# A decoder block on one core: the MLP's down product by seven quarter-block products instead of eight

## The chip, the cores and the metric

The kernel runs on one core of one Trainium2 chip. The metric is the device time of one execution in microseconds (us), taken as a median over runs. TensorE multiplies into PSUM, VectorE and ScalarE do the elementwise work and can read PSUM, GpSimd does elementwise work on SBUF alone, and SyncE issues most of the loads.

## The reference

```python
def reference(x, ...):                       # x: 1 x 256 x 2048, float32
    h = rms_norm(x, g_mix); proj = h @ w_in  # q k v r lr cb cc cx ga gb
    ...                                      # gated linear attention, short convolution
    x = x + merged @ w_o
    h2 = rms_norm(x, g_ffn)
    hid = square(relu(h2 @ w_ffn_up))        # 256 x 8192
    x = x + hid @ w_ffn_down                 # 8192 x 2048
    return rms_norm(x, g_final)
```

Only the last three lines and the norm are touched by the change.

## The kernel before, in words

Every matrix product runs in split float32: an operand is cast to the matmul's own float format (`hi`), the rest is kept as `lo = x - hi`, and the product is the sum of hi·hi, hi·lo and lo·hi. So each weight tile is loaded by SyncE (1 MB), cast in two halves of 128x1024 by ScalarE (L52), and VectorE subtracts to get `lo` (L53); five `whi` and five `wlo` buffers let both run ahead of TensorE.

The MLP works in four quarters of 2048 hidden columns (L610). For each of 16 blocks of 128 hidden columns, `ws_product` (L57) multiplies one up weight tile with the 16 activation tiles `B`: 16 matmuls of 512 columns and 16 of 256. `total` (L75) then adds main part and correction: ScalarE copies the correction out of PSUM (L78), VectorE adds (L79), squares the positive part (L614), and the result is split again into the tile `A[i]` (L86, L87). After 16 blocks `xs_product` (L129) multiplies the quarter by the down weights: for each of four column groups of 512, 16 blocks x 2 token halves x 3 matmuls of 512 columns (L415 to L417), two PSUM banks at a time. `down_evac` (L586) adds a bank to the residual `xtok` with one VectorE instruction (L589). The last column group of the last quarter is done one token half at a time (L644), followed by the final norm and the store.

The order on each engine is made by a scheduler that reorders the instructions of the program by its own priorities; a pool with n buffers limits how far a producer runs ahead. GpSimd does nothing but set four constants.

Of the kernel before, what the change touches and what calls it, by code (L numbers as in the profile page):

```python
# [20 lines left out]
GATE_NORM = 16.0  # L21
LEVELS = (4, 8, 16, 32, 64)
NM = len(LEVELS) * 64 + 128 + 3 * 64
NQ = 4


@with_exitstack
def block_kernel(ctx, tc, xT, wq, wk, wlr, wv, wr, wcb, wcc, wcx, wga, wgb, wgu,
# [557 lines left out]
    def down_evac(ps, m, c0, w, k):  # L586

        xs = xtok[:, m, c0:c0 + w]
        nc.vector.scalar_tensor_tensor(out=xs, in0=ps, scalar=rs2[:, m:m + 1], in1=xs, op0=ALU.mult, op1=ALU.add)  # L589
        if k is not None:  # L590
            jk = mp.tile([P, 512], F32, tag="junk", name="jk")
            nc.scalar.activation(jk[:, :w], xs, AF.Square, accum_out=ssq[:, m, k:k + 1])
            if k < 3:
                nc.vector.tensor_mul(out=xs, in0=xs, in1=gf[:, c0:c0 + w])

    def final_norm(m):
        nc.vector.tensor_reduce(out=sqf[:, m:m + 1], in_=ssq[:, m, :4 + m], op=ALU.add, axis=mybir.AxisListType.X)
        nc.vector.tensor_scalar(out=msf[:, m:m + 1], in0=sqf[:, m:m + 1], scalar1=1.0 / D, scalar2=EPS,
                                op0=ALU.mult, op1=ALU.add)
        rf = rsqrt_mean(msf[:, m:m + 1], [P, 1], "rf", 2)  # L600
        for c in range(4):
            xs = xtok[:, m, c * 512:(c + 1) * 512]
            if c < 3:
# [4 lines left out]
            nc.sync.dma_start(out=out[m * P:(m + 1) * P, c * 512:(c + 1) * 512], in_=xs)

    for qd in range(NQ):  # L610
        for i in range(KT):
# [1 line left out]
            hid = tmp("t1")
            nc.vector.scalar_tensor_tensor(out=hid, in0=s, scalar=0.0, in1=s, op0=ALU.max, op1=ALU.mult)  # L614
            split_act(A[i], hid)
        final = qd == NQ - 1
        for c in range(4):
            if final and c == 3:
                break
# [7 lines left out]
    for kg in range(4):
        src = wdown[((NQ - 1) * 4 + 3) * 4 + kg]  # L630
        if kg < 2:
            st = wst.tile([P, 2048], F32, tag="wst", name="wst_t")
            nc.sync.dma_start(out=st, in_=src)
            for kk in range(4):
                hi, lo = B[(kg * 4 + kk) * 2], B[(kg * 4 + kk) * 2 + 1]
                ws = st[:, kk * 512:(kk + 1) * 512]
                nc.scalar.copy(out=hi, in_=ws)
                nc.vector.tensor_sub(out=lo, in0=ws, in1=hi.bitcast(F32))
                wres.append((hi, lo))
        else:  # L640
            for hi, lo in wsplit(src):
                for kk in range(2):
                    wres.append((hi[:, kk * 512:(kk + 1) * 512], lo[:, kk * 512:(kk + 1) * 512]))
    for m in range(2):  # L644
        for c0, cw_ in ((0, 512),) if m == 0 else ((0, 256), (256, 256)):
            ps = mmp.tile([P, cw_], F32, tag="mm", name="ps_xs")
            for kt in range(KT):
# [1 line left out]
                ah = A[kt][:, m * P:(m + 1) * P]
                al = A[kt][:, T + m * P:T + (m + 1) * P]  # L650
                nc.tensor.matmul(ps, lhsT=ah, rhs=hi[:, c0:c0 + cw_], start=(kt == 0), stop=False)  # L651
                nc.tensor.matmul(ps, lhsT=ah, rhs=lo[:, c0:c0 + cw_], start=False, stop=False)  # L652
                nc.tensor.matmul(ps, lhsT=al, rhs=hi[:, c0:c0 + cw_], start=False, stop=(kt == KT - 1))  # L653
# [77 lines left out]
```

## Time and profile before

| | us |
|---|---|
| median of 3 runs (1757.11 to 1757.98) | 1757.19 |
| the profiled execution | 1757.05 |
| its span, first to last instruction | 1755.1 |
| TensorE busy in it | 1739.9 |
| VectorE / ScalarE / GpSimd busy | 1117.4 / 834.5 / 0.2 |

A busy time is the sum of an engine's instruction durations; matmul ends are modelled and matmuls overlap, so the rate of TensorE is read from start to start or from the length of a stretch. The granted clock was 1.00 in the stretches shown below.

### The profile page before, as it was taken

The page shows a single profiled execution, that of the slowest core. Times are in us where ns is not written, and L with a number is a line of the kernel's source. Part 1 is how long each engine was busy: PE and PEld are TensorE (multiplying, and loading weights), DVE is VectorE, ACT ScalarE, POOL GpSimd, SP SyncE. Part 2 cuts the span into 40 slices and gives each one's busy share as a digit, 9 for nine tenths or more (in the row PEclk, how much of TensorE's full clock was granted, in tenths as well). Part 3 has the DMA queues.
Part 4 walks back from the last instruction along what each step waited for, and adds up shares of the span by engine and source line. Part 5 has one row for each costly group of instructions (what it writes and reads, how often), then busy time and mean ns, then how long its engine had stood idle before and what let it go on. Part 6 is the DMA issues. An engine that isn't in the chain of part 4 may idle for free.

```text
span 1755.1 us, 22568 instructions
## 1 busy us (share of the span) xinstructions
PE 1739.9 (99%) x8988; PEld 1479.5 (84%) x8988; DVE 1117.4 (64%) x1597; ACT 834.5 (48%) x1098; POOL 0.2 (0%) x4
## 2 busy tenths in 40 slices
PE   8999999999999999999999999999999999999998
PEld 6888888888888888888888888888888888888887
DVE  8978888665544448864556666555665566556664
ACT  7745454444344446654444555434443444335451
POOL 0000000000000000000000000000000000000000
PEclk9999999999999999999999999999999999999999
DMA  8454444455555554465555555555555555555552
GB/s 314 168 192 169 168 168 168 169 191 192 192 192 192 192 192 148 171 211 195 193 191 202 205 188 192 190 193 192 186 179 196 193 184 191 192 192 192 186 191 79
DMA packets 74726, 328.72 MB, mean 187 GB/s; under 512 B 5693, under 2 KB 7869, under 8 KB 44158
## 3 DMA queue, kind: packets, MB, share of 16 engines
q1 hardware_dynamic: 71952, 323.55, 52.1%
q10 hardware_dynamic: 2670, 3.74, 0.6%
q8 instruction: 70, 1.15, 0.3%
q14 instruction: 34, 0.28, 0.0%
HBM read 325.17 MB, written 2.10 MB: 186 GB/s over the span
## 4 chain that ended last, share of the span: by engine, by line
PE 99%; DMA 0%; DVE 0%; ACT 0%; SPq 0%; issue 0%; DVEq 0%; ACTq 0%
PE ps_mm L70 34%; PE ps_mm L72 16%; PE ps_xs L415 8%; PE ps_xs L416 8%; PE ps_xs L417 8%; PE ps_xb L417 7%; PE ps_xb L415 7%; PE ps_xb L416 7%; PE ps_mm L69 1%; PE sp L289 1%; PE ps_mm L177 1%; PE ps_xs L652 0%; PE ps_xs L651 0%; PE ps_xs L653 0%; PE po L471 0%; PE ps_mm L179 0%
## 5 line engine op out<-in xcount | busy, mean ns | idle before, releaser
L53 DVE TENSOR_TENSOR wlo<-wst_t,whi 128x1024 fp32r<-128x1024 f32 x470 | 575.1, 1224 | 309.5 <-ACT whi L52 304.2
L52 ACT CAST whi<-wst_t 128x1024 fp32r<-128x1024 f32 x470 | 493.8, 1052 | 429.4 <-PE ps_xs L417 230.0
L70 PE MATMUL ps_mm<-A,whi 128*128 128x512 f32 x1488 | 527.1, 399 | 0.0
L72 PE MATMUL ps_mm<-A,wlo 128*128 128x256 f32 x1395 | 392.6, 281 | 0.0
L70 PE MATMUL ps_mm<-B,whi 128*128 128x512 f32 x1024 | 357.5, 399 | 0.0
L70 PEld LDWEIGHTS ps_mm<-A,whi 128*128 128x128 f32 x1488 | 275.8, 188 | 58.5
L72 PE MATMUL ps_mm<-B,wlo 128*128 128x256 f32 x960 | 269.7, 281 | 0.0
L72 PEld LDWEIGHTS ps_mm<-A,wlo 128*128 128x128 f32 x1395 | 263.3, 189 | 2.7
L442 DVE TENSOR_TENSOR wlo<-wst_t,whi 128x1024 fp32r<-128x1024 f32 x128 | 156.8, 1225 | 170.7 <-ACT whi L441 170.5
L415 PE MATMUL ps_xs<-whi,A 128*128 128x512 f32 x608 | 236.5, 389 | 0.0
L416 PE MATMUL ps_xs<-wlo,A 128*128 128x512 f32 x608 | 236.5, 389 | 0.0
L417 PE MATMUL ps_xs<-whi,A 128*128 128x512 f32 x608 | 236.5, 389 | 0.0
L70 PEld LDWEIGHTS ps_mm<-B,whi 128*128 128x128 f32 x1024 | 188.4, 188 | 41.7
L441 ACT CAST whi<-wst_t 128x1024 fp32r<-128x1024 f32 x128 | 134.8, 1053 | 184.6 <-PE ps_xb L417 174.6
L72 PEld LDWEIGHTS ps_mm<-B,wlo 128*128 128x128 f32 x960 | 181.3, 189 | 3.1
L78 ACT COPY corr<-ps_mm 128x256 f32<-128x256 f32 x144 | 53.6, 372 | 221.8 <-PE ps_mm L70 220.9
L417 PEld LDWEIGHTS ps_xs<-whi,A 128*128 128x128 f32 x608 | 114.2, 188 | 23.8
L415 PEld LDWEIGHTS ps_xs<-whi,A 128*128 128x128 f32 x608 | 114.2, 188 | 23.6
L416 PEld LDWEIGHTS ps_xs<-wlo,A 128*128 128x128 f32 x608 | 114.2, 188 | 23.5
L79 DVE TENSOR_TENSOR t<-ps_mm,corr 128x256 f32<-128x256 f32 x144 | 60.9, 423 | 108.2 <-ACT corr L78 107.6
L415 PE MATMUL ps_xb<-whi,A 128*128 128x512 f32 x256 | 99.9, 390 | 0.0
L415 PE MATMUL ps_xb<-whi,B 128*128 128x512 f32 x256 | 99.8, 390 | 0.0
(188 smaller groups left out, 1564.4 us busy)
## 6 DMA issues: line engine op xcount, KB each, us to landing
wst_t<-in_wup SPq DMA_DIRECT2D x64, 1024.0 KB, 4.8
wst_t<-in_wdown SPq DMA_DIRECT2D x64, 1024.0 KB, 4.8
wst_t<-in_wcc SPq DMA_DIRECT2D x16, 1024.0 KB, 4.8
wst_t<-in_wcx SPq DMA_DIRECT2D x16, 1024.0 KB, 4.8
wst_t<-in_wcb SPq DMA_DIRECT2D x16, 1024.0 KB, 4.8
wst_t<-in_wv SPq DMA_DIRECT2D x16, 1024.0 KB, 4.7
wst_t<-in_wgb SPq DMA_DIRECT2D x16, 1024.0 KB, 5.0
wst_t<-in_wconv SPq DMA_DIRECT2D x16, 1024.0 KB, 5.0
```

The lines of the kernel that those rows point to most:

```text
L52: nc.scalar.copy(out=hi, in_=s)
L53: nc.vector.tensor_sub(out=lo, in0=s, in1=hi.bitcast(F32))
L69: nc.tensor.matmul(ps[:, T:], lhsT=lo[:, sl], rhs=act[kt][:, :T], start=False, stop=False)
L70: nc.tensor.matmul(ps, lhsT=hi[:, sl], rhs=act[kt], start=(kt == 0), stop=last)
L72: nc.tensor.matmul(ps[:, T:], lhsT=lo[:, sl], rhs=act[kt][:, :T], start=False, stop=False)
L78: nc.scalar.copy(out=c, in_=corr)
L79: nc.vector.tensor_add(out=out_t, in0=main, in1=c)
L415: nc.tensor.matmul(pss[m], lhsT=ah, rhs=hi, start=(kt == 0), stop=False)
L416: nc.tensor.matmul(pss[m], lhsT=ah, rhs=lo, start=False, stop=False)
L417: nc.tensor.matmul(pss[m], lhsT=al, rhs=hi, start=False, stop=(kt == n - 1))
L441: nc.scalar.copy(out=hi, in_=sh)
L442: nc.vector.tensor_sub(out=lo, in0=sh, in1=hi.bitcast(F32))
```

## The change

The MLP now goes in eight pieces of 1024 hidden columns. For pieces 1 to 7 the down product is made of *units*: a unit is 512 hidden columns (`d`) by 1024 output columns (`g`), four units a piece. Left operand (256 tokens x 512), right operand (512 x 1024) and result are cut in 2x2 quarter blocks, and a unit is seven products of quarter blocks, 6 matmuls of 512 columns each, where eight would be needed otherwise. The seven need sums of quarter blocks. Of the right side (`s_tiles`) they are `x1`, `x2`, an in-place sum in the loaded tile, and `x4`, each 128x1024 and made by GpSimd. Of the left side (`combos`) they are four, each 128x256, by GpSimd. The seven results lie in seven PSUM banks, and after the two units of a `g` they are combined into `xtok` (`s_evac`): VectorE and ScalarE read the banks, GpSimd does five additions of 128x512.

Between the seven products of a unit stand two up products of the next piece, in the eighth bank `f`; the second half of the second one's `lo` is subtracted by GpSimd instead of VectorE. Up weights are loaded in half tiles (`uraw`, 3 buffers). The residual is scaled at the start so that the additions need no scale. The eighth piece is multiplied in the old way. Tiles of earlier stages share memory with the new ones.

```diff
-NQ = 4
+CH = 8
+NC = 64 // CH
...
+    def up_product(src, tag, dst, pool_last):
+        ps = bank(tag)
+        for hf in range(2):
+            s = mp.tile([P, 1024], F32, tag="uraw", name="uraw", bufs=3)
+            nc.sync.dma_start(out=s, in_=src[:, hf * 1024:(hf + 1) * 1024])
...
+            nc.scalar.copy(out=hi, in_=s)
+            (nc.gpsimd if pool_last and hf == 1 else nc.vector).tensor_sub(out=lo, in0=s, in1=hi.bitcast(F32))
...
+    def combos(hr):
...
+        nc.gpsimd.tensor_sub(out=st[:, :, 0, :], in0=a21, in1=a22)
+        nc.gpsimd.tensor_sub(out=st[:, :, 2, :], in0=a11, in1=a21)
+        nc.gpsimd.tensor_sub(out=st[:, :, 1, :], in0=st[:, :, 0, :], in1=a11)
+        nc.gpsimd.tensor_add(out=st[:, :, 3, :], in0=a12, in1=st[:, :, 1, :])
+        for dst, src in ((slice(0, 1), hr[:, :, 0, 0:1, :]), (slice(1, 3), hr[:, :, 1, :, :]), (slice(3, 7), st)):
+            nc.scalar.copy(out=ah[:, :, dst, :], in_=src)
+            nc.vector.tensor_sub(out=al[:, :, dst, :], in0=src, in1=ah[:, :, dst, :].bitcast(F32))
...
+    def s_tiles(ws, ops, qs, first, last):
...
+        def step(src, left, ps):
...
+            nc.scalar.copy(out=hi, in_=src)
+            nc.vector.tensor_sub(out=lo, in0=src, in1=hi.bitcast(F32))
+            for kp in range(2):
+                nc.tensor.matmul(ps, lhsT=ah[:, kp, left, :], rhs=hi[:, kp, :], start=first and kp == 0, stop=False)
+                nc.tensor.matmul(ps, lhsT=ah[:, kp, left, :], rhs=lo[:, kp, :], start=False, stop=False)
+                nc.tensor.matmul(ps, lhsT=al[:, kp, left, :], rhs=hi[:, kp, :], start=False, stop=last and kp == 1)
...
+        nc.gpsimd.tensor_add(out=x1, in0=b11, in1=b12)
+        nc.gpsimd.tensor_add(out=x2, in0=x1, in1=b22)
+        step(b11, A11, q1)
+        step(b21, A12, q2)
+        step(b22, S4, q3)
+        step(x1, S5, q5)
+        nc.gpsimd.tensor_add(out=b12, in0=b12, in1=b22)
+        step(x2, S2, q6)
+        nc.gpsimd.tensor_add(out=x4, in0=x2, in1=b21)
+        step(b12, S3, q7)
+        step(x4, A22, q4)
...
+    def s_evac(banks, g):
...
+        nc.scalar.copy(out=c[:, 0, :], in_=q1)
+        nc.vector.tensor_add(out=z1, in0=q23, in1=z1)
+        nc.gpsimd.tensor_add(out=z1[:, :512], in0=z1[:, :512], in1=c[:, 0, :])
+        nc.vector.tensor_add(out=u[:, 0, :], in0=q6, in1=c[:, 0, :])
+        nc.gpsimd.tensor_sub(out=z1[:, 512:], in0=z1[:, 512:], in1=u[:, 0, :])
+        nc.vector.tensor_add(out=u[:, 1, :], in0=q7, in1=u[:, 0, :])
+        nc.scalar.copy(out=c[:, 1, :], in_=q5)
+        nc.vector.tensor_add(out=z2, in0=q45, in1=z2)
+        nc.gpsimd.tensor_add(out=z1[:, 512:], in0=z1[:, 512:], in1=c[:, 1, :])
+        nc.gpsimd.tensor_add(out=z2[:, :512], in0=z2[:, :512], in1=u[:, 1, :])
+        nc.gpsimd.tensor_sub(out=z2[:, 512:], in0=z2[:, 512:], in1=u[:, 1, :])
...
-    for qd in range(NQ):
-        for i in range(KT):
-            s = total(ws_product(wup[qd * KT + i], B), tmp("t0"))
...
-            pss = xs_product([wdown[(qd * 4 + c) * 4 + kg] for kg in range(4)], A)
-            for m in range(2):
-                down_evac(pss[m], m, c * 512, 512, c if final else None)
+    for c in range(NC - 1):
...
+        for g in range(2):
+            banks = s_banks()
+            for d in range(2):
...
+                s = s_tiles(down_load(c, g, d), ops[d], banks[2], d == 0, d == 1)
+                for n, w in ((2, True), (3, True), (2, False)):
+                    for _ in range(n):
+                        next(s)
+                    if w:
+                        up_product(wup[(c + 1) * CH + j], "f", hcol(nxt[j // 4], j % 4), j % 2 == 1)
+                        j += 1
+                if j % 4 == 0 and c < NC - 2:
+                    nops.append(combos(nxt[j // 4 - 1]))
+            s_evac(banks, g)
```

So TensorE's order in a unit is: two products (`b11`, `b21`), an up product, three products (`b22`, `x1`, `x2`), an up product, two products (`b12`, `x4`).

What the scheduler makes of it is shown at the turn from one pair of units to the next, at the end of a piece. First VectorE before, in a down product (`xs_product`) and the first up blocks after it; `ps_xs` are the two banks, `ps_mm` is an up block's bank.

```order
980 L53 TENSOR_TENSOR wlo<-wst_t,whi 128x1024 x8
981 L589 SCALAR_TENSOR_TENSOR xtok<-ps_xs,rs_8834,xtok 128x512 x2
982 L53 TENSOR_TENSOR wlo<-wst_t,whi 128x1024 x8
983 L589 SCALAR_TENSOR_TENSOR xtok<-ps_xs,rs_8834,xtok 128x512 x2
984 L53 TENSOR_TENSOR wlo<-wst_t,whi 128x1024 x2
985 L79 TENSOR_TENSOR t_10263<-ps_mm,corr 128x256
```

Now VectorE at a turn: L82 and L630 finish the last up product of the old pair, L719 and L721 read the old pair's banks, L650 splits the left sums for the next piece, and L677 makes the `lo` of the new unit's right operands (`x` are GpSimd's sums).

```order
969 L82 TENSOR_TENSOR t_10016<-ps_f,corr 128x256
970 L630 SCALAR_TENSOR_TENSOR hraw<-t_10016 128x256
971 L619 TENSOR_TENSOR wlo<-uraw,whi 128x1024
972 L719 TENSOR_TENSOR u_10056<-ps_q_9678,u_10056 128x512
973 L650 TENSOR_TENSOR al<-hraw,ah 128x2x128
974 L650 TENSOR_TENSOR al<-hraw,ah 128x2x256
975 L619 TENSOR_TENSOR wlo<-uraw,whi 128x1024
976 L650 TENSOR_TENSOR al<-st_s,ah 128x2x512
977 L721 TENSOR_TENSOR xtok<-ps_q_9675,xtok 128x1024
978 L677 TENSOR_TENSOR wlo<-wst_t,whi 128x1024
979 L677 TENSOR_TENSOR wlo<-x,whi 128x1024 x2
```

Where two lines alternated, nine instructions (969 to 977) now stand between the end of an up product and the `lo` of the new unit's third product, and the read of the banks of `q4` and `q5` (L721) comes after the splits L650. At the turn in the middle of a piece the three L650 are not there.

GpSimd had no work before. Its order at the same turn now (L644 to L647 are the left sums, L722 to L724 the last three additions into `xtok`, L684, L694 and L685 the new unit's `x1`, in-place sum and `x2`):

```order
51 L644 TENSOR_TENSOR st_s<-hraw 128x2x128
52 L646 TENSOR_TENSOR st_s<-st_s,hraw 128x2x128
53 L647 TENSOR_TENSOR st_s<-hraw,st_s 128x2x128
54 L722 TENSOR_TENSOR xtok<-xtok,c_10055 128x512
55 L723 TENSOR_TENSOR xtok<-xtok,u_10056 128x512
56 L724 TENSOR_TENSOR xtok<-xtok,u_10056 128x512
57 L684 TENSOR_TENSOR x<-wst_t 128x1024
58 L694 TENSOR_TENSOR wst_t<-wst_t 128x2x512
59 L685 TENSOR_TENSOR x<-x,wst_t 128x1024
60 L619 TENSOR_TENSOR wlo<-uraw,whi 128x1024
```

The new unit's sums stand behind the old pair's additions, and the in-place sum, which TensorE needs sixth, stands ahead of `x2`, which it needs fifth.

## Rows read from the trace of the kernel before

**Rows 1.** The page's busy time by engine, and its chain of waits by engine.

```profile
span 1755.1 us, 22568 instructions
PE 1739.9 (99%) x8988; PEld 1479.5 (84%) x8988; DVE 1117.4 (64%) x1597; ACT 834.5 (48%) x1098; POOL 0.2 (0%) x4
...
PE 99%; DMA 0%; DVE 0%; ACT 0%; SPq 0%; issue 0%; DVEq 0%; ACTq 0%
```

**Rows 2.** Stretches: a quarter's up products, its down product, the next up products.

```profile
core 0: us, PE busy (x) PEld busy (x) DVE busy (x) ACT busy (x) POOL busy (x), PEclk, DMA share, GB/s
1213.13:1303.58 90.45, 90.45 (x513) 78.44 (x512) 58.15 (x79) 43.78 (x62) 0.00 (x0) 1.00 0.53 186
1303.58:1390.61 87.03, 87.03 (x385) 72.10 (x384) 44.54 (x42) 34.41 (x34) 0.00 (x0) 1.00 0.55 193
1390.61:1481.07 90.46, 90.46 (x513) 78.43 (x512) 58.17 (x79) 43.78 (x62) 0.00 (x0) 1.00 0.52 186
```

**Rows 3.** Groups of VectorE and ScalarE: forms, count, busy us, mean ns, idle before.

```profile
L53 DVE TENSOR_TENSOR wlo<-wst_t,whi 128x1024 fp32r<-128x1024 f32 x470 | 575.1, 1224 | 309.5 <-ACT whi L52 304.2
L545 DVE TENSOR_TENSOR mg<-ps_xb,sga 128x512 f32<-128x512 f32 x8 | 5.4, 683 | 0.0
L546 DVE TENSOR_TENSOR mg<-mg,tb 128x512 f32<-128x512 f32 x8 | 5.4, 687 | 0.1
L79 DVE TENSOR_TENSOR t<-ps_mm,corr 128x256 f32<-128x256 f32 x144 | 60.9, 423 | 108.2 <-ACT corr L78 107.6
L614 DVE SCALAR_TENSOR_TENSOR t<-t 128x256 f32<-128x256 f32 x64 | 27.3, 426 | 2.2
L87 DVE TENSOR_TENSOR A<-t,A 128x256 fp32r<-128x256 f32 x64 | 26.9, 420 | 0.0
L52 ACT CAST whi<-wst_t 128x1024 fp32r<-128x1024 f32 x470 | 493.8, 1052 | 429.4 <-PE ps_xs L417 230.0 <-PE ps_mm L70 178.7 <-PE ps_xb L417 16.7
L78 ACT COPY corr<-ps_mm 128x256 f32<-128x256 f32 x144 | 53.6, 372 | 221.8 <-PE ps_mm L70 220.9 <-PE ps_mm L177 0.7
```

**Rows 4.** All that GpSimd (POOL) does, same columns.

```profile
L723 POOL MEMSET const-bfloat16-1.0<- 128x1 bf16 x1 | 0.1, 101 | 0.0
L723 POOL MEMSET const-float32-0.0<- 128x1 f32 x1 | 0.1, 98 | 0.2 <-issue 0.2
```

**Rows 5.** Timeline round the end of an up product: start us, duration us, engine.

```profile
1046.71 0.63 PE L70 MATMUL ps_mm<-B,whi 128*128 128x512 f32 x2
1047.15 0.37 ACT L78 COPY corr<-ps_mm 128x256 f32<-128x256 f32 x1 [1.91 <-PE ps_mm L70]
1047.56 0.42 DVE L79 TENSOR_TENSOR t<-ps_mm,corr 128x256 f32<-128x256 f32 x1 [1.06 <-ACT corr L78]
1048.02 0.43 DVE L614 SCALAR_TENSOR_TENSOR t<-t 128x256 f32<-128x256 f32 x1
1048.51 1.23 DVE L53 TENSOR_TENSOR wlo<-wst_t,whi 128x1024 fp32r<-128x1024 f32 x1
```

**Rows 6.** The page's transfer rate in 40 slices, and two groups of loads.

```profile
GB/s 314 168 192 169 168 168 168 169 191 192 192 192 192 192 192 148 171 211 195 193 191 202 205 188 192 190 193 192 186 179 196 193 184 191 192 192 192 186 191 79
...
wst_t<-in_wup SPq DMA_DIRECT2D x64, 1024.0 KB, 4.8
wst_t<-in_wdown SPq DMA_DIRECT2D x64, 1024.0 KB, 4.8
```

More of the change, by code (lines that the diff above doesn't have):

```diff
@@ L98, in rsqrt_mean @@
         return y
-    A = [apool.tile([P, 512], F32R, tag=f"A{i}", name=f"A{i}") for i in range(KT)]
-    B = [apool.tile([P, 512], F32R, tag=f"B{i}", name=f"B{i}") for i in range(KT)]
+    SLOTS = {"hraw": 2, "x": 3, "st": 1, "ev": 2}
+    a2 = [apool.tile([P, 2, 512], F32R, tag=tag, name="A2", bufs=n) for tag, n in SLOTS.items() for _ in range(n)]
+    A = [a2[i // 2][:, i % 2, :] for i in range(KT)]
+    B = [bpool.tile([P, 512], F32R, tag=f"B{i}", name=f"B{i}") for i in range(KT)]
     colt = cpool.tile([P, 84], F32, name="colt")
@@ L584, in block_kernel @@
     msf = cpool.tile([P, 2], F32, name="msf")
+    def up_product(src, tag, dst, pool_last):
+        ps = bank(tag)
+        for hf in range(2):
+            s = mp.tile([P, 1024], F32, tag="uraw", name="uraw", bufs=3)
+            nc.sync.dma_start(out=s, in_=src[:, hf * 1024:(hf + 1) * 1024])
+            hi = wsp.tile([P, 1024], F32R, tag="whi", name="whi")
+            lo = wsp.tile([P, 1024], F32R, tag="wlo", name="wlo")
+            nc.scalar.copy(out=hi, in_=s)
+            (nc.gpsimd if pool_last and hf == 1 else nc.vector).tensor_sub(out=lo, in0=s, in1=hi.bitcast(F32))
+            for k8 in range(8):
+                kt = hf * 8 + k8
+                sl = slice(k8 * P, (k8 + 1) * P)
+                last = kt == KT - 1
+                if last:
+                    nc.tensor.matmul(ps[:, T:], lhsT=lo[:, sl], rhs=B[kt][:, :T], start=False, stop=False)
+                nc.tensor.matmul(ps, lhsT=hi[:, sl], rhs=B[kt], start=(kt == 0), stop=last)
+                if not last:
+                    nc.tensor.matmul(ps[:, T:], lhsT=lo[:, sl], rhs=B[kt][:, :T], start=False, stop=False)
+        s = total((ps[:, :T], ps[:, T:]), tmp("t0"))
+        nc.vector.scalar_tensor_tensor(out=dst, in0=s, scalar=0.0, in1=s, op0=ALU.max, op1=ALU.mult)
@@ new lines, in block_kernel, with down_load @@
+    A11, A12, A22, S5, S2, S3, S4 = range(7)
+    def down_load(c, g, d):
+        kt = c * CH + d * 4
+        tiles = []
+        for n in range(2):
+            st = wst.tile([P, 2, 2, 512], F32, tag="wst", name="wst_t")
+            nc.sync.dma_start(out=st.rearrange("p a b n -> p (a b n)"),
+                              in_=wdown[(kt // KT * 4 + 2 * g + n) * 4 + kt % KT // 4])
+            tiles.append(st)
+        return tiles
+    def s_tiles(ws, ops, qs, first, last):
+        ra, rb = ws
+        b11, b21, b12, b22 = ra[:, :, 0, :], ra[:, :, 1, :], rb[:, :, 0, :], rb[:, :, 1, :]
+        ah, al = ops
+        x1, x2, x4 = (apool.tile([P, 2, 512], F32, tag="x", name="x", bufs=3) for _ in range(3))
+        def step(src, left, ps):
+            hi = wsp.tile([P, 2, 512], F32R, tag="whi", name="whi")
+            lo = wsp.tile([P, 2, 512], F32R, tag="wlo", name="wlo")
+            nc.scalar.copy(out=hi, in_=src)
[4 more added lines that the diff above has]
+                nc.tensor.matmul(ps, lhsT=al[:, kp, left, :], rhs=hi[:, kp, :], start=False, stop=last and kp == 1)
+        q1, q2, q3, q4, q5, q6, q7 = qs
+        nc.gpsimd.tensor_add(out=x1, in0=b11, in1=b12)
+        nc.gpsimd.tensor_add(out=x2, in0=x1, in1=b22)
+        step(b11, A11, q1)
+        yield
+        step(b21, A12, q2)
+        yield
+        step(b22, S4, q3)
+        yield
+        step(x1, S5, q5)
+        yield
+        nc.gpsimd.tensor_add(out=b12, in0=b12, in1=b22)
+        step(x2, S2, q6)
+        yield
+        nc.gpsimd.tensor_add(out=x4, in0=x2, in1=b21)
+        step(b12, S3, q7)
+        yield
+        step(x4, A22, q4)
+        yield
@@ new lines, in s_banks @@
+    def s_banks():
+        q23 = ps7.tile([P, 1024], F32, tag="q23", name="ps_q23")
+        q45 = ps7.tile([P, 1024], F32, tag="q45", name="ps_q45")
+        return q23, q45, (bank("q1"), q23[:, :512], q23[:, 512:], q45[:, :512], q45[:, 512:], bank("q6"), bank("q7"))
+    def s_evac(banks, g):
+        q23, q45, (q1, _, _, _, q5, q6, q7) = banks
+        z1, z2 = (xtok[:, m, g * 1024:(g + 1) * 1024] for m in range(2))
+        c = apool.tile([P, 2, 512], F32, tag="ev", name="c15", bufs=2)
+        u = apool.tile([P, 2, 512], F32, tag="ev", name="u23", bufs=2)
+        nc.scalar.copy(out=c[:, 0, :], in_=q1)
[9 more added lines that the diff above has]
+        nc.gpsimd.tensor_sub(out=z2[:, 512:], in0=z2[:, 512:], in1=u[:, 1, :])
@@ new lines, in block_kernel @@
+    for m in range(2):
+        nc.vector.tensor_scalar(out=xtok[:, m, :], in0=xtok[:, m, :], scalar1=ms2[:, m:m + 1], scalar2=None,
+                                op0=ALU.mult)
+    hid = [hidden_tile(), hidden_tile()]
+    for j in range(CH):
+        up_product(wup[j], ("f", "q1", "q6", "q7")[j % 4], hcol(hid[j // 4], j % 4), False)
+    ops = [combos(h) for h in hid]
+    for c in range(NC - 1):
+        nxt, nops = [], []
+        j = 0
+        for g in range(2):
+            banks = s_banks()
+            for d in range(2):
+                if j % 4 == 0:
+                    nxt.append(hidden_tile())
+                s = s_tiles(down_load(c, g, d), ops[d], banks[2], d == 0, d == 1)
[8 more added lines that the diff above has]
+            s_evac(banks, g)
+        hid, ops = nxt, nops
@@ new lines, in block_kernel @@
+    gf = [apool.tile([P, 2, 512], F32, tag="x", name="gf", bufs=3) for _ in range(2)]
+    for i in range(2):
+        nc.scalar.dma_start(out=gf[i].rearrange("p c n -> p (c n)"), in_=gfin[:, i * 1024:(i + 1) * 1024])
+    act = []
+    for h in hid:
+        hf_ = h.rearrange("p a b m t -> p (a b m t)")
+        ah = mp.tile([P, 1024], F32R, tag="ah", name="ah_l", bufs=2)
+        al = mp.tile([P, 1024], F32R, tag="al", name="al_l", bufs=2)
+        nc.scalar.copy(out=ah, in_=hf_)
+        nc.vector.tensor_sub(out=al, in0=hf_, in1=ah.bitcast(F32))
+        act += [(ah[:, i * T:(i + 1) * T], al[:, i * T:(i + 1) * T]) for i in range(4)]
@@ L586, in down_evac, with last_mm @@
+    def last_mm(ps, m, kt, hi, lo):
+        ah, al = (a[:, m * P:(m + 1) * P] for a in act[kt])
+        nc.tensor.matmul(ps, lhsT=ah, rhs=hi, start=(kt == 0), stop=False)
+        nc.tensor.matmul(ps, lhsT=ah, rhs=lo, start=False, stop=False)
+        nc.tensor.matmul(ps, lhsT=al, rhs=hi, start=False, stop=(kt == CH - 1))
     def down_evac(ps, m, c0, w, k):
         xs = xtok[:, m, c0:c0 + w]
-        nc.vector.scalar_tensor_tensor(out=xs, in0=ps, scalar=rs2[:, m:m + 1], in1=xs, op0=ALU.mult, op1=ALU.add)
@@ L590, in down_evac @@
[L590 to L594, printed above, removed]
+        nc.vector.tensor_add(out=xs, in0=ps, in1=xs)
+        jk = apool.tile([P, 512], F32, tag="ev", name="jk", bufs=2)
+        nc.scalar.activation(jk[:, :w], xs, AF.Square, scale=rs2[:, m:m + 1], accum_out=ssq[:, m, k:k + 1])
@@ L596, in final_norm @@
+        if k < 3:
+            nc.vector.tensor_mul(out=xs, in0=xs, in1=gf[c0 // 1024][:, c0 // 512 % 2, :w])
     def final_norm(m):
@@ L605, in final_norm @@
             else:
-                nc.vector.scalar_tensor_tensor(out=xs, in0=xs, scalar=rf, in1=gf[:, c * 512:(c + 1) * 512],
+                nc.vector.scalar_tensor_tensor(out=xs, in0=xs, scalar=rf, in1=gf[1][:, 1, :],
                                                op0=ALU.mult, op1=ALU.mult)
             nc.sync.dma_start(out=out[m * P:(m + 1) * P, c * 512:(c + 1) * 512], in_=xs)
-    for qd in range(NQ):
-        for i in range(KT):
-            s = total(ws_product(wup[qd * KT + i], B), tmp("t0"))
[L613 to L619, printed above, removed]
-            pss = xs_product([wdown[(qd * 4 + c) * 4 + kg] for kg in range(4)], A)
-            for m in range(2):
-                down_evac(pss[m], m, c * 512, 512, c if final else None)
-            if final and c == 0:
-                nc.scalar.activation(warm[:, 1:2], ssq[:, 0, 0:1], AF.Sqrt)
@@ L628, in block_kernel, with last_weights @@
-    wres = []
[L629 to L643, printed above, removed]
+    def last_weights(c):
+        return [wdown[(3 * 4 + c) * 4 + kg] for kg in (2, 3)]
@@ new lines, in block_kernel @@
+    for c in range(3):
+        pss = [bank(("f", "q1", "q6", "q7")[(2 * c + m) % 4]) for m in range(2)]
+        for kg, src in enumerate(last_weights(c)):
+            halves = wsplit(src)
+            for kk in range(4):
+                hi, lo = halves[kk // 2]
+                sl = slice((kk % 2) * 512, (kk % 2 + 1) * 512)
+                for m in range(2):
+                    last_mm(pss[m], m, kg * 4 + kk, hi[:, sl], lo[:, sl])
+        for m in range(2):
+            down_evac(pss[m], m, c * 512, 512, c)
+        if c == 0:
+            nc.scalar.activation(warm[:, 1:2], ssq[:, 0, 0:1], AF.Sqrt)
@@ L644, in block_kernel @@
+    wres = []
+    for src in last_weights(3):
+        for hi, lo in wsplit(src):
+            for kk in range(2):
+                wres.append((hi[:, kk * 512:(kk + 1) * 512], lo[:, kk * 512:(kk + 1) * 512]))
     for m in range(2):
         for c0, cw_ in ((0, 512),) if m == 0 else ((0, 256), (256, 256)):
-            ps = mmp.tile([P, cw_], F32, tag="mm", name="ps_xs")
-            for kt in range(KT):
+            ps = bank(("q6", "q7", "f")[m + c0 // 256])[:, :cw_]
+            for kt in range(CH):
@@ L648, in block_kernel @@
                 hi, lo = wres[kt]
[L649 to L653, printed above, removed]
+                last_mm(ps, m, kt, hi[:, c0:c0 + cw_], lo[:, c0:c0 + cw_])
```

45 lines of the change are left out of this document (32 added, 13 removed).

## The prediction

> **What bounds the kernel now.** I read the page's busy times and the chain of waits first [rows 1]. TensorE is busy 1739.9 of 1755.1 us, and the chain that ended last lies on it for 99%. So time goes down only where TensorE issues less, and goes up where it waits. Next the stretches of the MLP [rows 2]: a quarter's 16 up products take 90.45 us, 5.653 us each, and its down product 87.03 us for 4 x 16 x 2 x 3 = 384 matmuls, 0.2266 us each. VectorE is busy for 58.2 and 44.5 us there, ScalarE for 43.8 and 34.4, so nothing else comes near. Then the groups of VectorE and ScalarE for the price of one instruction [rows 3]: both have long idle stretches ahead of them, VectorE 309.5 us at L53, as they wait for each other and for buffers. GpSimd does only four constants of one column [rows 4].
>
> **What it removes.** A piece of 1024 hidden columns cost 192 down matmuls; it now costs 4 units x 7 products x 6 = 168. Seven pieces change: 7 x 24 x 0.2266 = 38.1 us less on TensorE, all of it on the path [rows 1, 2]. The up products keep their 32 matmuls. The profiled execution took 1757.05 us (median of the runs 1757.19, so nothing is to be corrected), and without a new wait it would take 1719.0.
>
> **What it adds beside TensorE.** A piece now needs 8 x 5.653 + 168 x 0.2266 = 83.3 us of TensorE; before it was (90.45 + 87.03) / 2 = 88.7. Per piece, with [rows 3]:
> - VectorE: 12 up and 28 unit subtractions of 128x1024 at 1.224 (49.0), 8 totals and squares at 0.423 and 0.426 (6.8), the left splits 2 x (0.420 + 0.687 + 1.224) = 4.7, four bank reads of 1024 at about 1.22 and four of 512 at 0.683 (7.6): 68.1 us.
> - ScalarE: 44 casts at 1.052 (46.3), the rest copies and small casts (some 10): 56 us.
> - GpSimd: 16 right sums and 4 up subtractions of 128x1024, 10 additions of 512, 8 left sums of 256: as much as 27 operations of 128x1024.
>
> GpSimd's price p for one such operation of two operands stands in no row [rows 4]. The nearest row is VectorE's same operation, 1.224 us [rows 3]; that is the low end, both operands streamed at once. The high end is 2.45 us, two such passes, the operands one after the other; two ScalarE passes of 1.052 would make 2.10. I take 2.45: L53 shows that VectorE streams two operands in one pass, no row shows it of another engine, and ScalarE's rows all read one. Either way GpSimd's sum (33 to 66 us) fits under 83.3, as VectorE's and ScalarE's do. On sums alone everything is hidden, and the question is where the engines wait for each other in their order.
>
> [...]
>
> **The wait it adds.** At a turn from one pair of units to the next, GpSimd's order has the old pair's last two additions (L723, L724), then the new `x1`, the in-place sum, then `x2`. The additions wait for VectorE's read of the bank of `q4` (L721), the last product of the old pair. Behind them queue the new sums, behind those ScalarE's casts and VectorE's subtractions of `x1` and `x2`, for which TensorE waits. Count from zero, when TensorE goes on to the new unit. It has work without GpSimd for two products (2.72), an up product (5.65) and the third (1.36): `x1` is wanted at 9.73, `x2` at 11.09.
>
> VectorE's way to L721: the last up product ended at -2.72 (12 matmuls earlier); its copy starts 0.2 after the next product's first matmul (the second of the two from 1046.71, to 1047.15), and VectorE is through with total and square 1.36 after that (1048.51) [rows 5], so at -1.16. Then an up subtraction 1.22, a bank read of 512 (0.68), splits 0.42 and 0.69, an up subtraction 1.22, a split 1.22 and L721 1.22: done at 5.52. In the middle of a piece the three splits (2.33) are absent: 3.19. Then GpSimd needs p for two additions of 512, and 3p to the end of `x2`; cast and subtraction 2.27. So `x2` is ready at 7.79 + 4p at the end of a piece and 5.46 + 4p in its middle, and TensorE waits 4p - 3.30 or 4p - 5.63. For p = 2.45 that is 6.5 and 4.2 us. There are 6 turns of the first kind (the last piece splits nothing) and 7 of the second: 52p - 59.2 = 68.2 us. With 2.10 it is 50.0; with 1.224 only the first kind waits, 6 x 1.6 = 9.6. The gain is used up at p = 1.87.
>
> **What I cost at nothing.** Loads: 16.8 MB a piece in 83.3 us is 201 GB/s, where the first slice moved 314; and a unit's 4 MB, at 4.8 us a MB one after the other, take 19.2 of its 20.8 us [rows 6]. The start: VectorE scales the residual (at most 2 x 4 x 0.687 = 5.5 us), but the `lo` of two and a half up products (14.1 us of TensorE) stand ahead of it in its order. A bank's reuse: the new unit's first two banks are read on VectorE and ScalarE well ahead of zero. The tail is the same kind of work on half the blocks. I leave all of it at 0, bounds -2 and +5.
>
> **Forecast:** 1719.0 + 68.2 = 1787 us, slower, from p = 2.45; own range 1765 (p = 2.10) to 1830, if GpSimd also loses some 3 us a turn to VectorE.
>
> **Rival A, the sums are cheap.** If GpSimd streams both operands as VectorE does, p = 1.224: 1719.0 + 9.6 = 1728.6, faster. For it: four engines' sums fit, and most turns have slack then. Against: it needs p under 1.87, and only one engine's rows show such a pass.
>
> **Rival B, VectorE and GpSimd exclude each other.** If an instruction of VectorE with two SBUF operands can't run beside a sum of GpSimd, their times add: VectorE's such instructions are 49.0 + 3.4 (squares) + 4.7 = 57.1 us a piece, GpSimd's 27p. That is 123.3 us at p = 2.45 and 90.1 even at 1.224, over TensorE's 83.3 at once, so it decides from any price on. Against 88.7 before: 7 x 34.5 = 242, so 1999; at the low price 7 x 1.4, so 1767. The profile has nothing for or against, since GpSimd never ran beside VectorE [rows 4]; a part of it would land between 1787 and 1999.
>
> [...]
>
> **Rival C, a draw:** p near 1.87 or stalls that fall out a few us shorter, within 3.5 us of before, 1757.
>
> **Chances.** The forecast 0.42, rival B 0.28, rival A 0.24, the draw 0.06. A measurement of this kernel tells 0.2% (3.5 us) from no change: faster 0.24, same 0.06, slower 0.70. The range goes from 1730, where about the lower third of rival A is left out, to 1960, where the upper part of B is, together some 0.18.
>
> **What would show it.** Right: TensorE's matmuls of a unit still 0.2266 us apart; gaps ahead of the products of `x1` and `x2` in the first unit of each pair, released by VectorE's `lo`, that by ScalarE, that by GpSimd; L685 ending about 4p after L721; GpSimd's operation of 1024 near 2.45 us; other products without a gap. Rival A: that operation near 1.2. Rival B: L677's subtractions longer than 1.224, or GpSimd's operations spread far, and gaps at every product. Wrong: the step most at risk is p, since 0.1 us of it moves the sum by 5.2; next is VectorE's way to L721, 13 us per us.

## The result, and the profile after

The changed kernel takes 1938.78 us (median, 1938.65 to 1939.19), the kernel before 1757.15 beside it: a ratio of 1.103, 95% interval 1.101 to 1.105, so 181.6 us slower. The forecast was 1787, so 30 us slower: the side was right, and the size was six times too small.

The page after, busy times, three rows of 40 slices (PEclk is TensorE's granted clock, in tenths) and the chain (it answers to [rows 1]). DVE is VectorE, ACT ScalarE, POOL GpSimd and PE TensorE:

```profile
PE 1768.5 (91%) x8796; PEld 1477.1 (76%) x8796; DVE 1542.5 (80%) x1666; ACT 933.0 (48%) x1190; POOL 644.8 (33%) x270
...
DVE  8978887655444598445667899999999999999996
...
POOL 0000000000000000000002597777787787797750
PEclk9999999999999999999999999989889898898999
...
PE 66%; POOL 20%; DVE 7%; issue 4%; ACT 2%; DMA 1%; POOLq 0%; SPq 0%; DVEq 0%; ACTq 0%
```

VectorE is at 90% or more in the 16 slices from GpSimd's first full one to the last but one, and a third of the chain has left TensorE. The groups of VectorE, then of GpSimd (form, count, busy us, mean ns, idle before; they answer to [rows 3, 4]):

```profile
L677 DVE TENSOR_TENSOR wlo<-wst_t,whi 128x1024 fp32r<-128x1024 f32 x112 | 265.5, 2389 | 1.6 <-ACT whi L676 1.5
L677 DVE TENSOR_TENSOR wlo<-x,whi 128x1024 fp32r<-128x1024 f32 x84 | 183.9, 2209 | 1.6 <-ACT whi L676 1.6
L630 DVE SCALAR_TENSOR_TENSOR hraw<-t 128x256 f32<-128x256 f32 x64 | 77.9, 1218 | 2.2
L82 DVE TENSOR_TENSOR t<-ps_f,corr 128x256 f32<-128x256 f32 x58 | 24.0, 414 | 19.5 <-ACT corr L81 19.5
L721 DVE TENSOR_TENSOR xtok<-ps_q,xtok 128x1024 f32<-128x1024 f32 x14 | 17.0, 1216 | 0.0
```

```profile
L684 POOL TENSOR_TENSOR x<-wst_t 128x1024 f32<-128x1024 f32 x28 | 86.4, 3085 | 1142.0 <-DVE wlo L619 1035.6
L685 POOL TENSOR_TENSOR x<-x,wst_t 128x1024 f32<-128x1024 f32 x28 | 82.8, 2958 | 1.2 <-DVE wlo L677 1.2
```

The subtraction that took 1224 ns takes 2389, the square that took 426 takes 1218. But an instruction of VectorE with one operand in PSUM has not grown: L82 takes 414, where the same addition took 423 [rows 3], and L721 takes 1216, as in the run below in which GpSimd is idle (1217). Of the costly groups only those with both operands in SBUF have grown. The timeline at a place where both engines have work (start, duration), GpSimd and then VectorE:

```profile
1463.50 2.41 POOL L684 TENSOR_TENSOR x<-wst_t 128x1024 f32<-128x1024 f32 x1 [7.03 <-DVE wlo L677]
1465.99 3.27 POOL L694 TENSOR_TENSOR wst_t<-wst_t 128x1024 f32<-128x1024 f32 x1
1469.21 3.40 POOL L685 TENSOR_TENSOR x<-x,wst_t 128x1024 f32<-128x1024 f32 x1
```

```profile
1463.62 3.37 DVE L677 TENSOR_TENSOR wlo<-x,whi 128x1024 fp32r<-128x1024 f32 x1 [0.20 <-ACT whi L676]
1466.92 3.42 DVE L619 TENSOR_TENSOR wlo<-uraw,whi 128x1024 fp32r<-128x1024 f32 x1
1470.27 0.41 DVE L82 TENSOR_TENSOR t<-ps_f,corr 128x256 f32<-128x256 f32 x1
1470.71 2.19 DVE L630 SCALAR_TENSOR_TENSOR hraw<-t 128x256 f32<-128x256 f32 x1
1472.82 1.21 DVE L715 TENSOR_TENSOR xtok<-ps_q,xtok 128x1024 f32<-128x1024 f32 x1
1473.95 3.19 DVE L677 TENSOR_TENSOR wlo<-wst_t,whi 128x1024 fp32r<-128x1024 f32 x1
```

L684 ends at 1465.91, and VectorE's L677, begun at 1463.62, ends at 1466.99, 1.08 us after that. L694 ends at 1469.26, 2.27 us after L677; L619 ends at 1470.34, 1.08 after L694. Each waits for the whole of the other, 3.35 us a pair (1466.99 to 1470.34), though nothing of the program orders them. L82 in between passes in 0.41.

TensorE's waits in the changed kernel (us in total, times, longest), and the starts of the read of the old pair's banks, two a piece (min/median/max ns, first and last start):

```profile
PE ps_f L628 <- POOL wlo L619: 108.9, 26, 7.7
PE ps_f L626 <- DVE t L82: 21.3, 12, 2.2
PE ps_q L680 <- DVE wlo L677: 16.3, 22, 1.5
```

```profile
L721 DVE TENSOR_TENSOR xtok<-ps_q,xtok x14: 1212/1216/1219, 1141.9 to 1885.1; 128x1024 f32<-128x1024 f32 x14
```

13 half pieces in 743.2 us are 114.3 us a piece, against 88.7 before [rows 2]: 7 x 25.6 = 179 us, all of the loss but 2.

### The profile page after: what moved, and what is told of

Same layout as the page of the kernel before. It is cut to its first block, busy times and chain, and to the rows that moved or that the text cites. A ratio compares the mean times of both kernels' runs of the same rounds, so it can differ in the third digit from the quotient of the medians.

```text
span 1936.8 us, 22885 instructions
## 1 busy us (share of the span) xinstructions
PE 1768.5 (91%) x8796; PEld 1477.1 (76%) x8796; DVE 1542.5 (80%) x1666; ACT 933.0 (48%) x1190; POOL 644.8 (33%) x270
## 3 DMA queue, kind: packets, MB, share of 16 engines
q8 instruction: 69, 1.13, 0.2%
## 4 chain that ended last, share of the span: by engine, by line
PE 66%; POOL 20%; DVE 7%; issue 4%; ACT 2%; DMA 1%; POOLq 0%; SPq 0%; DVEq 0%; ACTq 0%
PE ps_mm L73 17%; PE ps_mm L75 8%; PE ps_xb L424 6%; PE ps_xb L422 6%; PE ps_xb L423 6%; PE ps_f L626 4%; DVE wlo L677 4%; POOL x L684 3%; POOL wlo L619 3%; POOL wst_t L694 3%; PE ps_f L628 2%; POOL x L685 2%; POOL xtok L724 2%; PE ps_xs L424 2%; PE ps_xs L423 1%
## 5 line engine op out<-in xcount | busy, mean ns | idle before, releaser
L684 POOL TENSOR_TENSOR x<-wst_t 128x1024 f32<-128x1024 f32 x28 | 86.4, 3085 | 1142.0 <-DVE wlo L619 1035.6
L626 PE MATMUL ps_f<-B,whi 128*128 128x512 f32 x928 | 366.1, 428 | 21.9 <-DVE t L82 21.3
L56 DVE TENSOR_TENSOR wlo<-wst_t,whi 128x1024 fp32r<-128x1024 f32 x234 | 288.2, 1235 | 102.3 <-ACT whi L55 100.9
L628 PE MATMUL ps_f<-B,wlo 128*128 128x256 f32 x870 | 264.8, 304 | 111.2 <-POOL wlo L619 108.9
L628 PEld LDWEIGHTS ps_f<-B,wlo 128*128 128x128 f32 x870 | 180.6, 208 | 124.3 <-POOL wlo L619 117.3
L677 DVE TENSOR_TENSOR wlo<-wst_t,whi 128x1024 fp32r<-128x1024 f32 x112 | 265.5, 2389 | 1.6 <-ACT whi L676 1.5
L626 PEld LDWEIGHTS ps_f<-B,whi 128*128 128x128 f32 x928 | 191.7, 207 | 69.5 <-DVE t L82 27.2
L619 DVE TENSOR_TENSOR wlo<-uraw,whi 128x1024 fp32r<-128x1024 f32 x100 | 179.1, 1802 | 10.0 <-ACT whi L618 9.1
L677 DVE TENSOR_TENSOR wlo<-x,whi 128x1024 fp32r<-128x1024 f32 x84 | 183.9, 2209 | 1.6 <-ACT whi L676 1.6
L680 PE MATMUL ps_q<-wlo,ah 128*128 128x512 f32 x392 | 158.3, 404 | 16.3 <-DVE wlo L677 16.3
L618 ACT CAST whi<-uraw 128x1024 fp32r<-128x1024 f32 x128 | 134.5, 1051 | 48.0 <-PE ps_f L626 31.1
L679 PE MATMUL ps_q<-whi,ah 128*128 128x512 f32 x392 | 156.3, 399 | 0.0
L681 PE MATMUL ps_q<-whi,al 128*128 128x512 f32 x392 | 154.6, 394 | 0.0
```

The source lines that it names most:

```text
L56: nc.vector.tensor_sub(out=lo, in0=s, in1=hi.bitcast(F32))
L619: (nc.gpsimd if pool_last and hf == 1 else nc.vector).tensor_sub(out=lo, in0=s, in1=hi.bitcast(F32))
L626: nc.tensor.matmul(ps, lhsT=hi[:, sl], rhs=B[kt], start=(kt == 0), stop=last)
L628: nc.tensor.matmul(ps[:, T:], lhsT=lo[:, sl], rhs=B[kt][:, :T], start=False, stop=False)
L677: nc.vector.tensor_sub(out=lo, in0=src, in1=hi.bitcast(F32))
L679: nc.tensor.matmul(ps, lhsT=ah[:, kp, left, :], rhs=hi[:, kp, :], start=first and kp == 0, stop=False)
```

## The experiments

Theory 1 is the prediction's rival B: VectorE's instructions with two SBUF operands and GpSimd's sums exclude each other. Theory 2: other traffic of the new order (loads, casts) stretches VectorE. Theory 3: the forecast's own waits at the turns. To compare them, one stretch of all kernels, 1131 to 1400 us, is used (busy us of each engine, granted clock, DMA share, GB/s): before, and after.

```profile
1131.00:1400.00 269.00, 269.00 (x1313) 226.71 (x1312) 149.98 (x165) 114.43 (x132) 0.00 (x0) 1.00 0.54 192
```

```profile
1131.00:1400.00 269.00, 215.48 (x977) 174.47 (x978) 260.22 (x161) 120.33 (x141) 218.55 (x91) 0.91 0.42 148
```

### The kernel before, with additions that nobody waits for

```diff
+    ga = mp.tile([P, 1024], F32, name="ga")
+    gb = mp.tile([P, 1024], F32, name="gb")
+    nc.gpsimd.memset(ga, 1.0)
+    extra += [lambda: nc.gpsimd.tensor_add(out=gb, in0=ga, in1=ga)] * 2   # issued at each of 126 weight tiles
```

> The kernel before, with 252 additions of 128x1024 on GpSimd (two operands in SBUF, a tile of their own that nobody reads) that run freely beside its last stages; no other instruction waits for them. Exclusion: while they run, VectorE's subtraction L53 (1224 ns in the kernel before) is held up by one addition each time, so its mean goes to between 2.4 and 3.6 us and the pair takes 2.42 + 1.14 = 3.56 us; a quarter's 64 subtractions then need 228 us against the quarter's 177.5, some 50 us more a quarter for about 4 quarters: 1850 to 1960. Without exclusion (GpSimd's sums cost only by the waits for them): 1757, L53 at 1.22.

Measured: 1931.18 us, ratio 1.099 (1.097 to 1.101). In the stretch from 1000 to 1600 us, VectorE's subtraction (L53 before) and GpSimd's addition:

```profile
L57 DVE TENSOR_TENSOR wlo<-wst_t,whi 128x1024 fp32r<-128x1024 f32 x156 | 425.3, 2754 | 0.0
...
L617 POOL TENSOR_TENSOR gb<-ga 128x1024 f32<-128x1024 f32 x233 | 578.0, 2481 | 18.3
```

252 additions, on which no instruction depends, cost 174 us. Theory 3 can't do that, and there is no new order of loads or casts for theory 2. VectorE pays: 2754 ns, while GpSimd's additions take 2481, little more than the 2.42 us of a sum that nothing holds up (measured below).

### The same with instructions that only write

```diff
+    extra += [lambda: nc.gpsimd.memset(gb, 0.0)] * 4
```

> The kernel before, with 504 GpSimd instructions that only write (128x1024, a constant) and that nobody waits for. If GpSimd's reads are what excludes VectorE's second operand: no change, 1757, L53 at 1.22. If any work of GpSimd does it, or its writes: L53 longer, above 1770.

Measured: 1756.99 us, ratio 1.000 (0.999 to 1.001), with GpSimd busy for 482.9 us:

```profile
L57 DVE TENSOR_TENSOR wlo<-wst_t,whi 128x1024 fp32r<-128x1024 f32 x470 | 575.0, 1224 | 309.2 <-ACT whi L56 304.1
...
L617 POOL MEMSET gb<- 128x1024 f32 x504 | 481.8, 956 | 28.9
```

So neither GpSimd's being busy nor its writing excludes VectorE. What an addition has beyond these instructions is its two reads and the arithmetic on them; a GpSimd instruction with one read wasn't tried.

### The changed kernel with writes in place of the sums

```diff
-        nc.gpsimd.tensor_add(out=x1, in0=b11, in1=b12)
-        nc.gpsimd.tensor_add(out=x2, in0=x1, in1=b22)
+        nc.gpsimd.memset(x1, 0.0)
+        nc.gpsimd.memset(x2, 0.0)
...
```

> The changed kernel with each of GpSimd's sums replaced by an instruction that only writes a constant to the same place (the sums are left out, so the output is not the reference's); the dependences between engines stay. Exclusion by reads: VectorE's subtractions back at 1.22 us and about the time of the kernel without sums, 1733, up to 1745. Exclusion by any GpSimd work: subtractions above 1.5 us, above 1780.

Measured: 1732.52 us, ratio 0.986 (0.984 to 0.987).

```profile
1131.00:1400.00 269.00, 269.00 (x1359) 226.29 (x1358) 208.00 (x222) 168.84 (x196) 83.62 (x120) 1.00 0.59 199
```

TensorE is full again, and VectorE's subtractions (L680, L622 in that run) are back at 1222 to 1223 ns. GpSimd writes to the same places and most of its waits are still there. What is gone are the reads, the waits for what was read, and the length of a sum: a write of 128x1024 takes 0.96 us, a sum 2.42.

### No sums at all

```diff
-        nc.gpsimd.tensor_add(out=x1, in0=b11, in1=b12)
...
-        step(x1, S5, q5)
+        step(b11, S5, q5)
```

> No sums at all: the seven products take the loaded blocks themselves, the left blocks are copied without sums, the bank reads add nothing on GpSimd (output is not the reference's); GpSimd is idle in the MLP, VectorE keeps its 68.1 us a piece. All theories but other traffic: TensorE alone bounds, 83.3 us a piece, 1719 as in the first term of the sum. Other traffic: subtractions above 1.8 us, above 1800.

Measured: 1732.99 us, ratio 0.986 (0.984 to 0.988). This is what the change brings without its sums: 24 us gained, not 38. VectorE's subtractions are at 1220 to 1223 ns. TensorE has no gap in the stretch; its piece takes 84.2 us instead of 83.3:

```profile
L709 DVE TENSOR_TENSOR xtok<-ps_q,xtok x14: 1215/1217/1219, 1131.3 to 1678.7; 128x1024 f32<-128x1024 f32 x14
```

7 x (88.7 - 84.2) = 31.5; the other 7 us are lost outside these pieces. Some 5 of them are lost ahead of the MLP: the last block of the residual is transposed on TensorE at 1036.8 us in the kernel before (L568) and at 1041.6 here (L575). Early in this run TensorE also has a wait of 2.3 us for a `lo` (L56) that the kernel before doesn't have. What causes the 5 us wasn't tried, and where the other 2 go is not settled.

### VectorE's subtractions with one operand

```diff
-            nc.vector.tensor_sub(out=lo, in0=src, in1=hi.bitcast(F32))
+            one(lo, hi.bitcast(F32))
...
+    def one(dst, src):
+        nc.vector.tensor_scalar(out=dst, in0=src, scalar1=0.5, scalar2=0.0, op0=ALU.mult, op1=ALU.add, accum_out=acc)
```

> The subtractions for lo on VectorE (L677, L619) become an instruction of the same length with one SBUF operand (it halves hi, with an accumulator; so lo and the output are wrong numbers); GpSimd's sums, their order and all waits stay. Exclusion: GpSimd's 128x1024 sums fall from 3.09 to about 2.3 us and the VectorE instruction is about 1.2; nothing adds up any more. The forecast's own waits at the turns are then what is left: with p = 2.27, 1719 + 52 x 2.27 - 59.2 = 1778; if those waits don't exist either, 1719. Other traffic: VectorE's instruction is still above 1.8 us and the time stays above 1880.

Measured: 1741.94 us, ratio 0.991 (0.990 to 0.993). All of GpSimd's sums are made, with all their waits, and yet:

```profile
1131.00:1400.00 269.00, 265.00 (x1335) 222.41 (x1334) 219.48 (x346) 166.90 (x193) 213.39 (x120) 1.00 0.53 191
```

```profile
L638 DVE TENSOR_SCALAR_CACHE_REDUCE wlo<-whi 128x1024 fp32r<-128x1024 f32 x296 | 360.2, 1217 | 61.5 <-ACT whi L684 24.4 <-ACT whi L618 16.6 <-DVE wlo L638 0.9
L633 DVE SCALAR_TENSOR_TENSOR hraw<-t 128x256 f32<-128x256 f32 x64 | 54.1, 846 | 2.2
```

```profile
L692 POOL TENSOR_TENSOR x<-wst_t 128x1024 f32<-128x1024 f32 x28 | 67.8, 2423 | 1120.2 <-DVE wlo L638 1035.0 <-ACT whi L684 85.1
L705 POOL TENSOR_TENSOR x<-x,wst_t 128x1024 f32<-128x1024 f32 x28 | 67.7, 2417 | 0.0
```

The same length of VectorE work on one operand runs beside the sums at 1217 ns, and the sums take 2.42 us: this is p. The square, which still has two operands, is still held up (846). Exclusion is confirmed, and the forecast falls: with p = 2.42 its waits should have made 1786. TensorE's waits in the stretch from 1131 to 1679:

```profile
PE ps_f L631 <- POOL wlo L620: 8.0, 6, 1.3
```

None of them is at a product of `x1` or `x2`, and they are nearly all of the 9 us that this run takes beyond the one without sums. At the end-of-piece turn that the trace shows here, the new pair's first unit begins about 1385.5, 12 matmuls before the up product from 1388.33. GpSimd, ScalarE, and TensorE's first matmul of the third product:

```profile
1379.25 2.40 POOL L705 TENSOR_TENSOR x<-x,wst_t 128x1024 f32<-128x1024 f32 x1
...
1390.99 2.42 POOL L692 TENSOR_TENSOR x<-wst_t 128x1024 f32<-128x1024 f32 x1
```

```profile
1387.17 1.05 ACT L684 CAST whi<-x 128x1024 fp32r<-128x1024 f32 x1
1388.53 1.05 ACT L684 CAST whi<-x 128x1024 fp32r<-128x1024 f32 x1 [0.31 <-PE ps_q L689]
```

```profile
1393.98 0.39 PE L687 MATMUL ps_q<-whi,ah 128*128 128x512 f32 x1
```

`x1` and `x2` of this unit are cast at 1387.17 and 1388.53, before GpSimd makes the next `x1` at 1390.99. So the `x1` that stands behind the old pair's additions is that of the pair's second unit: GpSimd runs a whole unit (21 us) ahead. The trace of the changed kernel itself shows the same: when GpSimd comes to the last addition of the first pair (L724, 1147.88) it has made three `x1` (L684), at that of the second pair (1205.93) five, at that of the third (1262.94) seven, each time one more than the two units of every finished pair. The account of the turn given with the change, that the new unit's sums stand behind the old pair's additions, is wrong by one unit.

### Only the up products' subtractions back on VectorE

```diff
-            (nc.gpsimd if pool_last and hf == 1 else nc.vector).tensor_sub(out=lo, in0=s, in1=hi.bitcast(F32))
+            nc.vector.tensor_sub(out=lo, in0=s, in1=hi.bitcast(F32))
```

> Only the quarter of the up products' subtractions that GpSimd had (4 a piece) goes back to VectorE; GpSimd keeps the sums. Exclusion: each moved one costs 1.22 us in place of 2.27 of the same shared time, 4 x 7 x 1.05 = 29 us less than the changed kernel: about 1910. The forecast's pacing: TensorE's waits for that instruction, 108.9 us in the changed kernel's list of waits, go: about 1830.

Measured: 1901.50 us, ratio 1.082 (1.081 to 1.084): 37 less than the changed kernel. Exclusion said 29, the forecast's waits 109. With the prices measured since, 2.42 for the moved subtraction on GpSimd and 1.13 from start to start on VectorE, exclusion gives 4 x 7 x 1.29 = 36, an estimate. That TensorE's list of waits put 108.9 us on this instruction meant only that it stood where the shortage came to light.

### All sums on VectorE

```diff
-        nc.gpsimd.tensor_add(out=x1, in0=b11, in1=b12)
+        nc.vector.tensor_add(out=x1, in0=b11, in1=b12)
...
```

> VectorE makes all the sums that GpSimd made (27 operations of 128x1024 a piece more on VectorE), GpSimd does nothing in the MLP. Theory 1, exclusion (a VectorE instruction with two SBUF operands and a sum on GpSimd never run at once): the subtractions L677 and L619 go back from 2.2 to 1.22 us, VectorE's load is 68.1 + 27 x 1.224 = 101.2 us a piece against 114.3 measured in the changed kernel, so 1757 + 7 x (101.2 - 88.7) = 1844, some 20 more if turns wait; faster than the changed kernel though VectorE does more. Theory 2, other traffic (the subtractions are long because of loads and ScalarE's casts in the interleaved order, not because of GpSimd): they stay above 2 us, VectorE needs over 150 us a piece, above 2100. Theory 3, the forecast's pacing alone: no prediction of its own beside VectorE's load, also 1844 or more.

Measured: 1802.49 us, ratio 1.026 (1.024 to 1.027). Giving VectorE half as much work again (27 operations of 128x1024 a piece) gains 136 us over the changed kernel:

```profile
1131.00:1400.00 269.00, 243.60 (x1179) 202.21 (x1178) 263.93 (x305) 150.03 (x175) 0.00 (x0) 0.96 0.51 174
```

```profile
L677 DVE TENSOR_TENSOR wlo<-x,whi 128x1024 fp32r<-128x1024 f32 x84 | 101.0, 1217 | 0.0
```

```profile
L721 DVE TENSOR_TENSOR xtok<-ps_q,xtok x14: 1214/1220/1225, 1132.3 to 1749.0; 128x1024 f32<-128x1024 f32 x14
```

VectorE alone bounds, at 94.9 us a piece, not 101.2: an instruction recorded with 1.21 us lets the next start after 1.13 (1472.82 and 1473.95 in the timeline above).

### Versions between: some units by eight products, sums on VectorE

```diff
+        for src, lefts, pss, last in ((ra[:, :, 0, :], (A11, A21), (q2, q4), False), ...):   # 4 casts, 48 matmuls
...
-        nc.gpsimd.tensor_add(out=x4, in0=x2, in1=b21)
+        nc.vector.tensor_add(out=b21, in0=x2, in1=b21)
```

> A version for both limits: the sums on VectorE (GpSimd idle), and only the first unit of each pair by seven products, the second by eight, added into the banks of the third, second, fourth and fifth product (one split of 128x1024 for its left blocks; x4 made in the loaded tile; uraw 4 buffers). TensorE per piece: 84.0 (measured without sums) + 2 x 6 x 0.2266 = 86.7 us. VectorE per piece: 12 instead of 16 right sums and lo's fewer, between the 94.7 measured with all sums and the 50 of the old kernel, about 75. So TensorE bounds: 7 x (88.7 - 86.7) = 14 less than before, less the 9 that the kernel without sums lost outside the pieces: about 1752, between 1740 and 1760. If VectorE's order holds TensorE up at the Strassen units, 1760 to 1780.

Measured: 1752.90 us, ratio 0.998 (0.997 to 0.999). But this version adds the second unit's fourth block to the bank of the fifth product, which goes into two result blocks, so that block is counted in both. The next version keeps it apart:

> As the half version, but with the second unit's fourth block in the bank of the seventh product, which is read before it (the fifth product goes into two result blocks, so nothing may be added to it); the sums of the first unit's products are taken between the two units. One bank read of 512 more a pair on VectorE, hidden. TensorE per piece 86.7 us as there: 1752, between 1748 and 1757; slower than that only if the early bank reads hold up VectorE's subtractions.

Measured: 1755.72 us, ratio 0.9989 (0.9981 to 0.9998): 0.1%, under what counts as a difference here. TensorE is full in the stretch:

```profile
1131.00:1400.00 269.00, 269.00 (x1349) 225.74 (x1348) 243.25 (x279) 144.47 (x165) 0.00 (x0) 1.00 0.55 192
```

> Three of four units by seven products, sums on VectorE, uraw with 2 buffers for want of space. TensorE per piece 84.0 + 6 x 0.2266 = 85.4; VectorE per piece between the 94.7 measured with all four and about 79 with two: some 87. So VectorE is at the edge: 1743 if its idle stretches vanish and TensorE bounds, 1757 + 7 x (87 - 88.7) + 9 = 1754 if VectorE bounds, up to 1775 if the two load buffers hold up the up products.

Measured: 1768.58 us, ratio 1.006 (1.005 to 1.008). VectorE is busy for 262 of 269 us there and TensorE has gaps:

```profile
1131.00:1400.00 269.00, 264.17 (x1308) 219.63 (x1306) 262.03 (x307) 155.44 (x176) 0.00 (x0) 0.99 0.55 192
```

So no version found that makes the right sums beats the kernel before by a margin that counts.

## Why the prediction was wrong

- **The step that failed is the choice between its own turn waits and rival B.** "At a turn from one pair of units to the next, GpSimd's order has the old pair's last two additions (L723, L724), then the new `x1`": 68.2 us rested on that, and the run with one-operand subtractions shows 8.0 us of waits, none of them at `x1` or `x2`. The order was read rightly row by row, but assigned to the wrong unit: the three buffers of `x` let GpSimd run a unit ahead, which the reading never asked. VectorE's bank read there also ended at 2.9 us after zero (L729 in that run, 1387.18 + 1.22), not 5.52. That the forecast's side was right is luck: it came from waits that weren't there.
- **The term of the sum that was left at zero is VectorE's.** "On sums alone everything is hidden" assumed that VectorE's and GpSimd's work overlap, and VectorE's 68.1 us a piece took durations from rows in which GpSimd stood idle. Its 57.1 us with two SBUF operands and GpSimd's sums add up: 114.3 = 57.1 + 27p gives p = 2.12, an effective price between rival B's two bounds. It is fitted to the measured piece and so no test of its own; with that piece 1719.0 + 7 x (114.3 - 83.3) = 1936, against 1938.8 measured. A better test is the pair's 3.35 from the timeline: 27 pairs (90.5), the other 13 subtractions at 1.13 (14.7) and the squares and left splits (8.1) make 113 us a piece, an estimate, against 114.3. Rival B's full sum with p = 2.45 (1999) is 60 us over, since instructions that follow each other overlap a little: 1.22 and 2.42 on record, 3.35 as a pair.
- **Rival B was given only 0.28, with the words "The profile has nothing for or against".** No row showed the two engines side by side, so the 0.28 was the author's estimate. The runs speak for rival B: 252 additions that read cost 174 us, 504 instructions that only write cost nothing (ratio 1.000), and VectorE's one-operand instructions stay at 1217 ns. But rival B's "gaps at every product" didn't come: of TensorE's waits 108.9 us stand at the up product whose `lo` GpSimd makes.
- **The value of p was right.** 2.45 was taken from two VectorE passes; it is 2.42 where nothing holds it up. Whether GpSimd takes its operands one after the other, as the prediction argued, no run tests. Rival A (p under 1.87) and the draw fall with it.
- **The first term was too large.** -38.1 was forecast, -24.2 is what is left without sums. The products are 0.2329 us apart (14 steps from 1384.84 to 1388.10 in the one-operand run), not 0.2266, up to 1.1 us a piece. Some 7 us are lost outside the pieces, 5 of them ahead of the MLP, a stage in which the forecast put no loss; their cause stays open.
- **Of what was costed at nothing, the loads held:** they delay nothing in the runs without exclusion (TensorE full at 199 and 200 GB/s).

## What to carry to other kernels

Before sums or subtractions of SBUF tiles are moved to an idle GpSimd, add their time to VectorE's instructions with two SBUF operands as if both were one engine, and compare that sum with the bound; here a sum that cost 1.13 us on VectorE cost 2.1 us of the shared time on GpSimd (the effective p above). A duration read where the other engine was idle isn't the duration beside it: VectorE's subtraction went from 1224 to 2389 ns. And when a wait is built from a queue's order, first find out, by the buffers, for which step of the loop each instruction works.

## What the runs showed of the hardware

- Who pays differs. In the changed kernel both engines stretch, 3.35 us a pair. Beside free-running additions of one tile to itself the pair takes 2.85 (five subtractions in 14.25 us from 1298.50) and only VectorE's durations stretch (2754 ns in the mean, GpSimd's 2481). Why this pair is shorter wasn't tried.
- A small instruction loses most in proportion: the square of 128x256 went from 426 to 1218 ns in the mean, since it waits for a whole sum of 128x1024: the one shown above, begun at 1470.71, ends at 1472.90, 0.29 us after GpSimd's L685 (1469.21 + 3.40).
- TensorE's mean granted clock was lower where TensorE had waited: 0.91 in the changed kernel's stretch, of which it waited 20%, 0.96 with all sums on VectorE, where it waited 9%, and 1.00 in the stretches where it was full. What the lower clock added wasn't separated. VectorE, which bounds there, was without work for only 8.8 of the 269 us in the first of these stretches.
